# A two-layer retention and neighbourhood-attention block on one core: weighings of ada rows pinned to their written place on VectorE

## The chip, the cores and the metric

The kernel runs on one core of a Trainium2 chip. The core has a matrix engine (TensorE, PE in the profile), a vector engine (VectorE, DVE), an activation engine (ScalarE, ACT), a general engine (GpSimd, POOL) and a queue engine that here only issues transfers (SyncE, SP). Each of them works through its own list of instructions in the order of that list and waits where an operand is not there yet. The metric is the device time of one execution in microseconds, as a median over runs; lower is better.

## The reference

The computation is a small diffusion transformer: 256 latent tokens and 256 context tokens of width 1024, two layers, float32.

Every layer first makes modulation vectors: `silu(c) @ ada_w[i] + ada_b[i]` for the latent tokens and the same with `c_ctx` for the context, six vectors of 1024 each (shift, scale and gate for the mixer, and again for the MLP). Then

- layer 0, the retention mixer: q, k, v and a gate are projected from the modulated tokens by `ret_w_in` (1024 x 6144); four heads with 256 columns of q and k and 512 of v; scores weighted by a decay over distance, forward and backward, the context first and then the latent tokens with the context's state; each head's output is normalized over its 512 columns, multiplied by `silu(gate)`, and all heads go through `ret_w_o` (2048 x 1024);
- a layer norm over `ALPHA * x + gate * y`, a modulation, an MLP with squared ReLU (1024 to 4096 to 1024), and a second layer norm;
- layer 1, the neighbourhood mixer with 32 heads, and again an MLP, for the latent tokens alone.

The output is the 256 latent tokens.

## The kernel before

All matrix products run as three products of float32r pieces. A weight comes into one of four `raw` buffers (`rawp`, L138), ScalarE copies it into a `hi` tile, VectorE subtracts to get `lo`, and `mm3` (L174) multiplies hi by hi, hi by lo and lo by hi. `fetch` (L255) issues the load and the copy, `lows` (L277) the subtraction, and `take` (L282) does both until five units are there ahead of use (`WB = 5`, L135). Activations are split the same way (`split`, L170).

**Order.** The kernel is written with tiles, and a planner turns the text into one list for each engine. It goes by its own model of times: an engine takes, of the instructions whose inputs the model takes as ready, the one that is written first. So an instruction may be planned ahead of others that are written before it. `InOrder` (L74) wraps the engines: with `on` set, each instruction is tied behind the one written just before it on the same engine. SyncE is tied at the start (`PIN`), so loads are issued in written order; the opening stage and the passages around the layer norms are tied on other engines too. The tie goes one way: an untied instruction written later may still be planned earlier than a tied one.

**Layer 0, mixer (L1060 on).** All 512 tokens are handled together, in four token tiles of 128. A loop runs over the four heads. In head 0, q and v have been made by the opening stage. For each head: `proj_T` for q and k; a loop of four steps for the values (L1090); `masked_scores` (L1123); the gate of token tiles 0 and 1; the product of scores and values with its statistics for four token tiles (`po`, `bs`, `on`); the gates of token tiles 2 and 3 in one pass (`gates`, L1106), in whose midst `to_oT` (L1191) turns the head's output of token tiles 0 and 1 on TensorE (`pT`), copies it (`oh`, ScalarE) and takes the low part (`ol`, VectorE). Then comes the output projection: two halves of 512 columns, four token tiles each, 12 matmuls a tile into `pw`; `gated` (L736) multiplies by the gate row into `acc` on VectorE and `add_to` adds it to the residual on GpSimd. The turns of token tiles 2 and 3 stand after tiles 0 and 1 of the first half. In head 3 the output projection is a passage of its own in tied order, with the layer norm.

**The background stream (L532).** The modulation vectors that are needed later are made beside all this. `bg()` (L600) advances a generator by one step. A step loads the next row block of `ada_w` into a `raw` buffer (128 x 2 x 512, 512 KB) and deals with the block loaded before. For the first eight blocks TensorE does the product. For the other 24 blocks of layer 0, VectorE multiplies by a column of `silu(c)` and accumulates:

```python
for kk in range(2):
    for t in range(nt):
        weigh(spare(t), raw[:, kk, :], t, 2 * (n % 4) + kk, n % 4 == 0 and kk == 0)
```

That is four weighings a block (`strips<-rawa` in the profile, since the sums lie in the spare part of the strip tiles). After every fourth block a further step folds the two sums into `red` (`folded`, L456), and after eight the columns or the gate row are finished at the next call (`flush`). So each third of the modulation vectors takes ten calls, and the stream of layer 0 takes 39 calls (`bg_max`). For layer 1 the stream weighs into `acc` tiles, beside the MLP of layer 0.

The calls before: head 0 makes four in `proj_T`, two in the first gate, one after the scores, two in the second gate (nine in all), then one at the middle and one at the end of the second pair of gates, one behind it (L1205), and four in the output projection, after token tiles 1 and 3 of each half. Heads 1 and 2 make three in the loop of values (steps 1 to 3), one after each of gates 0 and 1, one at L1205, and four in the output projection. Head 3 makes the last three in its loop of values.

Of the kernel before, what the change touches and what calls it, by code (L numbers as in the profile page):

```python
# [104 lines left out]
def kernel(  # L105
# [23 lines left out]
    pe, act, dve, pool, sp = (  # L129
        InOrder(tc, getattr(nc, e), e in PIN)  # L130
        for e in ("tensor", "scalar", "vector", "gpsimd", "sync")
    )
# [19 lines left out]
    def nm(s):  # L152
        uid[0] += 1
        return f"{s}_{uid[0]}"

    def bank(s="ps"):
        return psp.tile([P, 512], F32, tag="ps", name=nm(s))
# [8 lines left out]
    def tsl(t):  # L166
        return slice(t * P, (t + 1) * P)
# [259 lines left out]
    def ada_bias(l, offs, nb):  # L427
        brow = scr("brow")
        ab = ada_b[l]
        for i in range(2):  # L430
            sp.dma_start(
                out=brow[64 * i : 64 * i + 64, :nb],
                in_=bass.AP(ab.tensor, ab.offset + offs[i], [[nb, 2], [0, 32], [1, nb]]),
            )
        return brow

    def ada_mm(pr, k, nb, rhs):

        lhsT = cT[:, k, :, :].rearrange("p a t -> p (a t)")
        for j in range(4):  # L440
            pe.matmul(
                pr[32 * j : 32 * j + 32, 0:nb],
                lhsT=lhsT,
                rhs=rhs(j),
                start=(k == 0),
                stop=(k == KC - 1),
                tile_position=(0, 32 * j),
            )

    def ada_row(pr, brow, nb, p0=0, p1=P, row=None):  # L450
        if row is None:
            row = smp.tile([P, 256], F32, tag="row", name=nm("row"), bufs=1)
        dve.tensor_add(out=row[p0:p1, :nb], in0=pr[p0:p1, 0:nb], in1=brow[p0:p1, :nb])
        return row

    def folded(red, acc, t, c0, n):  # L456

        dve.tensor_reduce(
            out=red[:, t, c0 // 32 : (c0 + n) // 32], in_=acc.rearrange("p (b i) -> p b i", i=32),
            axis=mybir.AxisListType.X, op=ALU.add, apply_transpose=True,  # L460
        )
# [44 lines left out]
    def on_pe(l, w, part):  # L506
        return (l, w, part) == (0, 0, 2)

    def bg_load(l, w, part, offs, n):

        if l == 1 or w == 0:
            return ada_load(l, n, offs)
        raw = rawp.tile([P, 2, 512], F32, tag="raw", name=nm("rawa"))
        w_ap = ada_w[l][256 * (n % 4) : 256 * (n % 4) + 256, offs[n // 4] : offs[n // 4] + 512]
        sp.dma_start(out=raw[:], in_=w_ap.rearrange("(k p) n -> p k n", p=P))
        return raw

    def weigh(acc, raw, t, k, first):

        col = scol[:, t, k : k + 1]  # L520
        if first:
            dve.tensor_scalar_mul(out=acc, in0=raw, scalar1=col)
        else:
            dve.scalar_tensor_tensor(out=acc, in0=raw, scalar=col, in1=acc, op0=ALU.mult, op1=ALU.add)
# [3 lines left out]
    def flush():  # L528
        while due:
            due.pop(0)()  # L530

    def bg_stream():  # L532


        plan = []
        for l, w, part in (
            [(0, 0, 2), (0, 1, 0), (0, 1, 1), (0, 1, 2)]
            + [(1, 0, 0), (1, 0, 1), (1, 0, 2), (1, 1, 0), (1, 1, 1), (1, 1, 2)]
        ):
            sh, sc, g = 3 * w * D, (3 * w + 1) * D, (3 * w + 2) * D  # L540
            offs = (sh + 512 * part, sc + 512 * part) if part < 2 else (g, g + 512)
            for n in range(KC):
                plan.append((l, w, part, offs, n))
        nxt = bg_load(*plan[0])
        yield
        for step, (l, w, part, offs, n) in enumerate(plan):
            raw = nxt
            if step + 1 < len(plan):
                nxt = bg_load(*plan[step + 1])

            nt = 2 if l == 0 or (w == 0 and part < 2) else 1
            if on_pe(l, w, part):
                if n == 0:
                    pr = bank("pada")
                if n == KC - 2:
                    brow = ada_bias(l, offs, 256)
                ada_mm(pr, n, 256, lambda j: raw[:, j // 2, (j % 2) * 256 : (j % 2 + 1) * 256])
                if n == KC - 1:
                    row = ada_row(pr, brow, 256)
                    for t in range(2):  # L560
                        pool.dma_start(
                            out=grow[l, w][t].rearrange("(j c) -> j c", j=4), in_=row[t:P:32, :]
                        )
                yield
                continue
            if n == 0:
                red = smp.tile([P, 2, 32], F32, tag="red", name=nm("red"), bufs=2)
            if l == 0:
                for kk in range(2):
                    for t in range(nt):  # L570
                        weigh(spare(t), raw[:, kk, :], t, 2 * (n % 4) + kk, n % 4 == 0 and kk == 0)
                if n % 4 == 3:
                    yield
                    for t in range(nt):
                        folded(red, spare(t), t, 512 * (n // 4), 512)
            else:
                if n == 0:
                    acc = slot(S_VL, [P, 2, D], F32, "acc")
                for t in range(nt):

                    dve.on = n == 0 and (w, part) == (0, 0)
                    weigh(acc[:, t], raw[:].rearrange("p a n -> p (a n)"), t, n, n == 0)
                    dve.on = False
                if n == KC - 1:
                    for t in range(nt):
                        folded(red, acc[:, t], t, 0, D)
            if n == KC - 1:
                if part < 2:
                    due.append(lambda a=(l, w, red, 4 * part, nt): ada_columns(*a))
                else:  # L590
                    due.append(lambda a=(l, w, red, nt): ada_gate(*a))
            yield
# [7 lines left out]
    def bg(n=1):  # L600
        for _ in range(n):
            if bg_done[0] < bg_max[0]:
                flush()
                bg_done[0] += 1
                next(bgs, None)
# [224 lines left out]
    def spare(t):  # L830
        return strips[t][:, 1536:2048]
# [238 lines left out]
    for h in range(RH):  # L1070
        last = h == RH - 1
        if h == 0:
            qkh = slot(S_TH, [P, 4, NT], F32R, "qkh")
            qkl = slot(S_TL, [P, 4, NT], F32R, "qkl")
            vh = slot(S_VH, [P, 4, DV], F32R, "vh")
            vl = slot(S_VL, [P, 4, DV], F32R, "vl")
            rotate(pq, qkh[:, 0:2], qkl[:, 0:2], True)
            evac_v(pv, vh, vl)
            act.on = True
            for a in range(2):  # L1080
                act.mul(out=RR[a][:], in_=RR[a][:], mul=ALPHA)
            act.on = False
            proj_T(qkh[:, 2:4], qkl[:, 2:4], True)
        else:
            qkh = slot(S_TH, [P, 4, NT], F32R, "qkh")
            qkl = slot(S_TL, [P, 4, NT], F32R, "qkl")
            proj_T(qkh[:, 0:2], qkl[:, 0:2])
            proj_T(qkh[:, 2:4], qkl[:, 2:4])
            vh = slot(S_VH, [P, 4, DV], F32R, "vh")
            vl = slot(S_VL, [P, 4, DV], F32R, "vl")  # L1090
            pv = [bank("pv") for _ in range(4)]
            for u in range(4):
                ((wh, wl),) = take(1)
                for t in range(4):
                    for kk in range(2):
                        k = 2 * u + kk
                        mm3(pv[t][:], hs(k, t * P, (t + 1) * P), (wh[:, kk, :], wl[:, kk, :]), k == 0, k == KC - 1)
                if u:
                    bg()
            evac_v(pv, vh, vl)  # L1100
        qh, ql, kh, kl = qkh[:, 0:2], qkl[:, 0:2], qkh[:, 2:4], qkl[:, 2:4]

# [88 lines left out]
        def to_oT(t):  # L1191
            pT = bank("pT")
            for i in range(4):
                pe.transpose(pT[:, tsl(i)], gs[:, t, tsl(i)], ident)
            pv_ = pT[:].rearrange("p (k t) -> p k t", k=4)
            act.copy(out=oh[:, :, tsl(t)], in_=pv_)
            dve.tensor_sub(out=ol[:, :, tsl(t)], in0=pv_, in1=oh[:, :, tsl(t)].bitcast(F32))

        between = {4: lambda: to_oT(0), 5: lambda: to_oT(1)}
        for t, pg in zip((2, 3), gates((2, 3), between)):  # L1200
            sg = scr("sg")
            act.activation(out=sg[:], in_=pg[:], func=AF.Silu)
            pool.tensor_mul(out=gs[:, t, :], in0=sg[:], in1=gs[:, t, :])
            if t == 2:
                bg()  # L1205

        bg_until(9)
        first_gate()
# [1014 lines left out]
```

## Time and profile before

| | before |
|---|---|
| median of 3 runs | 1208.73 us (1206.9 to 1209.21) |
| the profiled execution | 1205.15 us, span 1203.4 us |
| mean granted TensorE clock | 0.997 |
| TensorE busy | 1176.1 us (98%) |
| VectorE busy | 825.5 us (69%) |
| ScalarE busy | 477.8 us (40%) |
| GpSimd busy | 255.0 us (21%) |
| weighings of layer 0 | 96, from 89.5 to 373.5 us |
| low parts of the head outputs (`ol`) | 16, from 115.0 to 437.8 us |

A line of a timeline has the start, the duration, the engine, the line of the source, the operation, `out<-in` by the names of the tiles, the shapes, and how many instructions are merged; in brackets stands the idle time of that engine just before, and what ended it. Nearly all instructions have the line of the wrapper, L84, so groups are told apart by their tiles. A line of the waits has the waiting engine and tile, the releaser, the microseconds in sum, the number of waits, and the longest. A line of the windows has busy time of PE, PEld, DVE, ACT and POOL (with counts), then the granted clock, the share of the DMA engines and GB/s.

### The profile page before, as it was taken

Reading aid. Unit: us, or ns where it says so; the run is one execution under the profiler, and the core shown is the slowest. Engines: PE = TensorE matmul, PEld = TensorE weight load, DVE = VectorE, ACT = ScalarE, POOL = GpSimd, SP = SyncE. Lnnn points to the kernel's source line nnn. Section 1 sums busy time; section 2 is a strip of 40 time slices with the busy share of each in tenths; the row PEclk is TensorE's granted clock in tenths of the full one; section 3 lists DMA queues with packets and bytes.
Section 4 is the critical chain, followed back from the end, with each engine's and each line's share of the span. In section 5 each row is a group of like instructions: output and inputs, shape, how many; then the busy total and the mean of one; then the engine's idle time right before and its main releaser. Section 6 shows DMA issues by size and latency. Waiting matters only on the chain.

```text
span 1203.4 us, 17830 instructions
## 1 busy us (share of the span) xinstructions
PE 1176.1 (98%) x6867; PEld 986.4 (82%) x6867; DVE 825.5 (69%) x1307; ACT 477.8 (40%) x809; POOL 255.0 (21%) x390
## 2 busy tenths in 40 slices
PE   7999899999999999999999999999999999999997
PEld 5777788788878888888888888889778878999886
DVE  3778676768576478667876675578576688787445
ACT  3562122323222246442122333227466665666341
POOL 1103400420340131491203000122444431000001
PEclk9999999999999999999999999999999999999999
DMA  9766443344143123856566655546244335566660
GB/s 302 225 228 193 144 134 107 105 133 165 62 154 117 59 82 117 263 113 195 170 197 204 211 189 196 185 150 204 80 144 133 103 115 162 182 211 202 236 210 36
DMA packets 130265, 193.16 MB, mean 161 GB/s; under 512 B 9676, under 2 KB 73332, under 8 KB 130180
## 3 DMA queue, kind: packets, MB, share of 16 engines
q1 hardware_dynamic: 121796, 179.02, 46.1%
q0 software_dynamic: 7232, 10.44, 3.9%
q10 hardware_dynamic: 1152, 2.56, 0.7%
q8 instruction: 54, 0.88, 0.3%
q14 instruction: 31, 0.25, 0.1%
HBM read 187.15 MB, written 5.75 MB: 160 GB/s over the span
## 4 chain that ended last, share of the span: by engine, by line
PE 82%; DVE 8%; DMA 4%; issue 2%; ACT 2%; POOL 1%; SPq 0%; DVEq 0%; ACTq 0%; POOLq 0%
PE p L84 40%; PE pq L84 7%; PE pv L84 7%; PE pn L84 5%; PE pg L84 5%; PE pw L84 4%; PE pnv L84 4%; DMA rawa<-in_ada_w_dram 2%; DVE lo L84 2%; PE po L84 2%; PE ppt L84 2%; PE pS L84 1%; PE pqk L84 1%; PE pada L84 1%; PE pav L84 1%
## 5 line engine op out<-in xcount | busy, mean ns | idle before, releaser
L84 ACT CAST hi<-raw 128x1024 fp32r<-128x1024 f32 (+2 forms) x228 | 231.9, 1032 | 323.6 <-PE p L84 123.4
L84 DVE TENSOR_TENSOR lo<-raw,hi 128x1024 fp32r<-128x1024 f32 (+2 forms) x228 | 274.0, 1214 | 109.5 <-ACT hi L84 109.1
L84 PE MATMUL p<-hi,hid 128*128 128x512 f32 (+1 forms) x832 | 241.8, 374 | 0.0
L84 PEld LDWEIGHTS p<-hi,hid 128*128 128x128 f32 x832 | 152.2, 188 | 27.7
L84 PE MATMUL p<-hTh,lo 128*128 128x256 f32 (+1 forms) x512 | 167.5, 327 | 1.9 <-DVE lo L84 1.9
L84 PE MATMUL p<-hTh,hi 128*128 128x256 f32 (+1 forms) x512 | 167.9, 328 | 0.2 <-ACT hTh L84 0.2
L84 PE MATMUL p<-hTl,hi 128*128 128x256 f32 (+1 forms) x512 | 167.3, 327 | 0.4 <-DVE hTl L84 0.4
L84 PE MATMUL p<-lo,hid 128*128 128x512 f32 (+1 forms) x416 | 155.3, 373 | 0.0
L84 DVE SCALAR_TENSOR_TENSOR acc<-rawa,scol,acc 128x1024 f32<-128x1024 f32 x56 | 74.7, 1344 | 66.0 <-DMA rawa<-in_ada_w_dram 66.0
L84 POOL TENSOR_TENSOR R<-R,acc 128x512 f32<-128x512 f32 x40 | 63.2, 1596 | 209.9 <-DVE acc L84 209.8
L84 PEld LDWEIGHTS p<-hTh,lo 128*128 128x128 f32 x512 | 96.4, 188 | 11.2 <-DVE lo L84 2.5
L84 PEld LDWEIGHTS p<-hTl,hi 128*128 128x128 f32 x512 | 96.4, 188 | 9.5 <-DVE hTl L84 0.8
L84 PEld LDWEIGHTS p<-hTh,hi 128*128 128x128 f32 x512 | 96.3, 188 | 9.2 <-ACT hTh L84 0.4
L84 PEld LDWEIGHTS p<-lo,hid 128*128 128x128 f32 x416 | 78.4, 188 | 13.6
L84 ACT CAST hid<-r 128x256 fp32r<-128x256 f32 (+1 forms) x64 | 32.0, 500 | 109.9 <-DVE r L84 109.9
L84 DVE SCALAR_TENSOR_TENSOR strips<-rawa,scol,strips 128x512 f32<-128x512 f32 x84 | 66.8, 830 | 9.8 <-DMA rawa<-in_ada_w_dram 9.7
L84 POOL TENSOR_TENSOR rstd<-rstd,misc 128x1 f32<-128x1 f32 x28 | 18.8, 672 | 208.5 <-DVE rstd L84 207.2
L84 PE MATMUL pw<-hi,ol 128*128 128x512 f32 x128 | 51.0, 398 | 6.5 <-DVE ol L84 6.5
L84 ACT ACTIVATE s<-s,mn 128x512 f32<-128x512 f32 x64 | 45.5, 713 | 26.2 <-DVE mn L84 26.2
L84 PE MATMUL pw<-hi,oh 128*128 128x512 f32 x128 | 51.6, 403 | 0.0
L84 PE MATMUL pg<-hi,hTh 128*128 128x512 f32 x128 | 51.3, 401 | 0.0
L84 PE MATMUL pw<-lo,oh 128*128 128x512 f32 x128 | 50.5, 394 | 0.0
(238 smaller groups left out, 2288.3 us busy)
## 6 DMA issues: line engine op xcount, KB each, us to landing
raw<-in_mlp_w_dram SPq DMA_DIRECT2D x128, 512.0 KB, 4.5
rawa<-in_ada_w_dram SPq DMA_DIRECT2D x80, 512.0 KB, 3.9
raw<-in_ret_w_in_dram SPq DMA_DIRECT2D x42, 512.0 KB, 3.5
raw<-in_nat_w_in_dram SPq DMA_DIRECT2D x24, 512.0 KB, 5.1
rawq<-in_ada_w_dram SPq DMA_DIRECT2D x16, 512.0 KB, 6.4
raw<-in_ret_w_o_dram SPq DMA_DIRECT2D x16, 512.0 KB, 3.5
bias<-rpb_rows POOLq DMA_DIRECT2D x32, 128.0 KB, 2.9
raw<-in_nat_w_o_dram SPq DMA_DIRECT2D x8, 512.0 KB, 4.2
```

What stands on the lines that cost most here:

```text
L84: r = f(*args, **kwargs)
```

## The change

Three edits. The weighings of layer 0 are tied in written order on VectorE. The subtraction that makes `ol` is tied too, with the setting that was there restored behind it. And `bg()` is called in all four steps of the loop of values of heads 1 to 3, while the call behind the second pair of gates, in every head, is gone.

```diff
             if l == 0:
+                dve.on = True
                 for kk in range(2):
                     for t in range(nt):
                         weigh(spare(t), raw[:, kk, :], t, 2 * (n % 4) + kk, n % 4 == 0 and kk == 0)
+                dve.on = False
                 if n % 4 == 3:
                     yield
                     for t in range(nt):
...
                         mm3(pv[t][:], hs(k, t * P, (t + 1) * P), (wh[:, kk, :], wl[:, kk, :]), k == 0, k == KC - 1)
-                if u:
-                    bg()
+                bg()
             evac_v(pv, vh, vl)
...
             act.copy(out=oh[:, :, tsl(t)], in_=pv_)
+            pinned, dve.on = dve.on, True
             dve.tensor_sub(out=ol[:, :, tsl(t)], in0=pv_, in1=oh[:, :, tsl(t)].bitcast(F32))
+            dve.on = pinned
...
             pool.tensor_mul(out=gs[:, t, :], in0=sg[:], in1=gs[:, t, :])
-            if t == 2:
-                bg()
```

The calls after: head 0 makes one fewer, heads 1 and 2 as many as before with the first at step 0 of the loop of values, and head 3 makes the last four there. The count of instructions and of bytes is the same.

## The prediction

> **What bounds the kernel now.** I read the busy table first, then TensorE's waits, then the timelines of TensorE and VectorE around each wait, and last the issues of SyncE and the idle of the helpers. The busy table and TensorE's longest waits:
>
> ```profile
> span 1203.4 us, 17830 instructions
> PE 1176.1 (98%) x6867; PEld 986.4 (82%) x6867; DVE 825.5 (69%) x1307; ACT 477.8 (40%) x809; POOL 255.0 (21%) x390
> PE pw L84 <- DVE ol L84: 6.5, 4, 2.8
> PE p L84 <- DVE lo L84: 1.9, 3, 0.8
> ```
>
> TensorE works 1176.1 of 1203.4 us, so 27.3 us of idle is all that any reordering elsewhere can win, plus slow clock. The largest wait of the whole run is the third line: matmuls of the output projection (`pw`) wait four times, 6.5 us in sum, for `ol`, the low part of the turned head output. That is the tile that the change pins. The four on TensorE, in order of time (start, duration, [idle before <- releaser]), the first with the last matmul ahead of it:
>
> ```profile
> 119.27 0.40 PE L84 MATMUL pw<-lo,oh 128*128 128x512 f32 x1
> 121.53 0.50 PE L84 MATMUL pw<-hi,ol 128*128 128x512 f32 x1 [1.85 <-DVE ol L84]
> 130.52 0.61 PE L84 MATMUL pw<-hi,ol 128*128 128x512 f32 x1 [2.80 <-DVE ol L84]
> 134.27 0.39 PE L84 MATMUL pw<-hi,ol 128*128 128x512 f32 x1
> 134.49 0.39 PE L84 MATMUL pw<-hi,oh 128*128 128x512 f32 x1
> 235.37 0.50 PE L84 MATMUL pw<-hi,ol 128*128 128x512 f32 x1 [1.27 <-DVE ol L84]
> 337.99 0.50 PE L84 MATMUL pw<-hi,ol 128*128 128x512 f32 x1 [0.62 <-DVE ol L84]
> ```
>
> Two are in head 0, one in head 1, one in head 2. What VectorE did instead:
>
> ```profile
> 117.13 1.94 DVE L84 TENSOR_SCALAR strips<-rawa,scol 128x512 f32<-128x512 f32 x2 [1.42 <-DMA rawa<-in_ada_w_dram]
> ...
> 120.79 0.68 DVE L84 TENSOR_TENSOR ol<-pT,oh 128x512 fp32r<-128x512 f32 x1
> 121.39 0.73 DVE L84 SCALAR_TENSOR_TENSOR strips<-rawa,scol,strips 128x512 f32<-128x512 f32 x1
> ...
> 123.19 0.68 DVE L84 TENSOR_TENSOR acc<-pw,G 128x512 f32<-128x512 f32 x1
> 123.79 0.67 DVE L84 TENSOR_TENSOR ol<-pT,oh 128x512 fp32r<-128x512 f32 x1
> 127.19 2.08 DVE L84 SCALAR_TENSOR_TENSOR strips<-rawa,scol,strips 128x512 f32<-128x512 f32 x3 [2.73 <-DMA rawa<-in_ada_w_dram]
> 129.18 0.68 DVE L84 TENSOR_TENSOR acc<-pw,G 128x512 f32<-128x512 f32 x1
> 129.78 0.68 DVE L84 TENSOR_TENSOR ol<-pT,oh 128x512 fp32r<-128x512 f32 x1
> ...
> 232.04 2.08 DVE L84 SCALAR_TENSOR_TENSOR strips<-rawa,scol,strips 128x512 f32<-128x512 f32 x3 [1.30 <-DMA rawa<-in_ada_w_dram]
> ```
>
> The weighings (`strips<-rawa`) stand on VectorE ahead of work that the text of the kernel puts before them, and at 127.19 the engine sits idle 2.73 us for a row of ada weights, weighs three times (2.08 us), and only then makes `acc` and the `ol` on which TensorE has stood since 127.7. Head 1 repeats it at 232.04. By the calls of `bg()` the weighings at 117 to 135 belong to the second half of the output projection and to head 1's loop of values: they ran early because nothing held them.
>
> **The change part by part.** *Weighings held in order.* Each of the 96 weighings of layer 0 now follows what was written before it on VectorE. No instruction is added. In head 0 the row whose call stands in the output projection (after `ol` of token tile 3) can no longer stand before that `ol`; so the 2.73 us of idle and the 2.08 us of weighing leave its path. *`ol` held in order*: it stands behind the `acc` or the `ol` written before it, and the next weighings behind it. *The call moved*: the call at line 1205, behind the second pair of gates and ahead of the output projection, goes, and the loop of values of heads 1 to 3 gets one at its first step, so the output projection starts with no weighing in front of it in heads 1 and 2. In head 0 a call is lost, and the stream runs one call later until head 1's loop of values; the last call falls in head 3's loop either way.
>
> The terms, TensorE time saved if all four waits go: 1.85 + 2.80 + 1.27 + 0.62 = 6.54 us. To this comes the clock behind the 2.80 us wait:
>
> ```profile
> 130.00:132.00 2.00, 1.48 (x4) 1.18 (x5) 2.00 (x3) 0.00 (x0) 1.21 (x1) 0.69 0.00 0
> 132.00:134.00 2.00, 2.00 (x6) 1.52 (x6) 2.00 (x4) 1.04 (x1) 0.24 (x1) 0.50 0.52 160
> 134.00:136.00 2.00, 2.00 (x10) 1.67 (x9) 2.00 (x3) 1.05 (x1) 1.50 (x1) 0.96 0.29 102
> ```
>
> The third column from the right is the granted clock: 0.69, 0.50, 0.96. From 130.52 to 134.27 nine matmuls started in 3.75 us; at the 0.22 us of the step from 134.27 to 134.49 they take 1.98 us, so 1.75 us (rounded to 1.7) go with the wait. Sum 8.2 us.
>
> [...]
>
> What is moved also has to fit elsewhere. One weighing costs 0.75 us undisturbed:
>
> ```profile
> L84 DVE SCALAR_TENSOR_TENSOR strips<-rawa,scol,strips x84: 718/745/1780, 92.1 to 373.5; 128x512 f32<-128x512 f32 x84
> 116.06 2.73 POOL L84 TENSOR_TENSOR gs<-sg,gs 128x512 f32<-128x512 f32 x2 [4.65 <-ACT sg L84]
> 224.63 3.84 POOL L84 TENSOR_TENSOR gs<-sg,gs 128x512 f32<-128x512 f32 x2 [7.30 <-ACT sg L84]
> 179.37 1.22 DVE L84 TENSOR_TENSOR lo<-raw,hi 128x1024 fp32r<-128x1024 f32 x1 [2.78 <-ACT hi L84]
> 181.38 4.30 DVE L84 SCALAR_TENSOR_TENSOR strips<-rawa,scol,strips 128x512 f32<-128x512 f32 x6 [0.79 <-DMA rawa<-in_ada_w_dram]
> 207.32 0.70 DVE L84 BATCH_NORM_STATS2 bs<-po 128x6 f32<-128x512 f32 x1 [7.99 <-PE po L84]
> ```
>
> The four weighings put into the loop of values are 4 x 0.75 = 3.0 us; VectorE idled 2.78 + 0.79 = 3.57 us in that loop of head 1, and the low parts of weights made there are for the gates, written after the scores. I cost them at nothing; without that cover they would be 3.0 us a head at most. The two rows of the calls after gate tiles 0 and 1 now run where they are written: 8 x 0.75 = 6.0 us, against 7.99 us of idle before `bs`. Nothing.
>
> *Raw buffers.* Four are shared by weights and ada rows, and SyncE issues in written order. A row held until its call keeps its buffer:
>
> ```profile
> 89.15 4.74 SPq L84 DMA_DIRECT2D rawa<-in_ada_w_dram  x3
> 93.98 5.62 SPq L84 DMA_DIRECT2D raw<-in_ret_w_o_dram  x3
> rawa<-in_ada_w_dram SPq DMA_DIRECT2D x80, 512.0 KB, 3.9
> raw<-in_ret_w_o_dram SPq DMA_DIRECT2D x16, 512.0 KB, 3.5
> 186.85 5.88 SPq L84 DMA_DIRECT2D raw<-in_ret_w_o_dram  x3
> 116.62 1.04 ACT L84 CAST hi<-raw 128x1024 fp32r<-128x1024 f32 x1
> 119.24 0.59 ACT L84 CAST oh<-pT 128x512 fp32r<-128x512 f32 x1 [1.57 <-PE pT L84]
> ```
>
> Before, three rows and then three output weights left by 99.6 us, since the rows were weighed at once. Now three rows wait for their calls, which I estimate at about 108, 115 and 125 us. One output weight gets the fourth buffer; the second and third leave at about 111, when the first row is weighed, land 3.5 us later, and are needed for the second half, at about 128: covered. The fourth (the next head's q) leaves at about 118, lands at 122; its copy and its low part could be planned just ahead of `oh` and `ol` of tile 3, which would then wait: from nothing to 2.0 us (landing 122, copy 1.04, low part 1.2, `acc` 0.6, `ol` 0.68 gives 125.5 to 126.5; the matmul wants it at about 125). In head 0 a weighing also still meets POOL's two products (2.73 us there; where weighings met them in head 1, 3.84), which is up to 1.1 us on the chain to the next transposes, with about 1 us of slack. I take 0.7 of these 0 to 3.1 us, near the low end, because heads 1 and 2 have cover: the three output weights of head 1 left from 186.85 on, and the two rows whose buffers they may now wait for are weighed by about 205 (199.3, where VectorE's idle before `bs` began, and 6.0); landed by 209, they are wanted from 225 on.
>
> Sum: 8.2 - 0.7 = 7.5 us. The profiled run took 1205.15 us (span 1203.4 and 1.75 around it), 3.58 below the median of the runs, 1208.73. So 1197.6 against the profiled run, and on the median's scale 1208.73 - 7.5 = 1201.2 us. TensorE is the bound from 63 us to the end, so what it saves early stays saved.
>
> **The rivals.** *The waits shrink but come back elsewhere.* `ol` is then late behind low parts of weights or `acc` that were behind the weighings before. For it: the order of everything unpinned is still the planner's, which believes loads earlier than they land (the 2.73 us above). Against it: `ol` now stands directly behind the `acc` of one tile earlier, and that is ready about 1.6 us before it is needed. It would keep the two small waits and half of the first, with the clock gained: 8.2 - (1.27 + 0.62 + 0.9) = 5.4, or, if the 2.80 us gap only shrinks to 1.85, 2.7 us: 1203.3 to 1206.0.
>
> *No change.* Pinning does not move `ol`, or the planner shifts something after head 3 by as much. Each instruction added to a fixed order can only be asked to wait longer. Within 0.2% (2.4 us, about what a measurement of this kernel can tell from no change): 1206.3 to 1211.1.
>
> *Slower: ScalarE stands in front of a held load.* A row pinned behind the output chain holds a raw buffer; the next weight's load leaves that much later; ScalarE, which copies the weight (`hi`) and makes `oh` on one queue, waits for it with `oh` behind it, and so do `ol` and TensorE. For it: 116.62 and 119.24 above stand 1.6 us apart in that order. Against: by the estimate above the loads of heads 1 and 2 have some 16 us to spare (209 against 225). It decides from 8.2 / 3 = 2.7 us a head on; with a wait of one load (3.5 us) and the 1.7 us of clock behind it in each of three heads it costs 15.6 - 8.2 = 7.4 us: 1216.
>
> [...]
>
> **How the numbers follow.** Forecast with the waits gone 0.55 (own range 1198.7 to 1204.2: gains of 8.2 to 5, and the runs' spread, 1206.9 to 1209.21, about the median; the small clock gain, 0.04, is in it), partial 0.19, no change 0.10, slower 0.16. Faster is 0.74, same 0.10, slower 0.16. The range runs from 1198.7 to 1209.5: it takes in the forecast, the partial case and most of no change, and leaves out the slower case.
>
> **What would show it.** Right: no wait of `pw` for `ol` over 0.7 us, a granted clock of 1.00 through the output projection of head 0; no weighing on VectorE between the first and the last `ol` of heads 1 and 2; the first weighings at about 108 us instead of 89; the idle before the first `bs` of head 1 down from 7.99 to about 2. Wrong: `ol` behind a `lo` that waits for `hi`, ScalarE's `hi` waiting for a load between two `oh`, new waits of `pv`, `pS` or `po`, or the same TensorE idle moved past 470 us.

## The result, and the profile after

The changed kernel takes 1201.29 us (median of 5 runs, 1199.77 to 1201.89) against 1207.70 us for the kernel before (5 runs, 1206.28 to 1209.21). The ratio is 0.9946, with a 95% interval from 0.9935 to 0.9957: 0.54% faster. The forecast was 1201.2 us.

The two profiled executions are nearer to each other than the medians: spans of 1199.5 and 1203.4 us, 3.9 us apart, where the medians are 6.4 apart. The profiled run of the kernel before, 1205.15 us, lies below all five of its timed runs. So these two traces can account for 3.9 us; the rest is between runs.

From the page of the changed kernel, the span and the busy table, and from its waits those of TensorE:

```profile
span 1199.5 us, 17825 instructions
PE 1176.4 (98%) x6867; PEld 987.8 (82%) x6867; DVE 832.7 (69%) x1307; ACT 477.6 (40%) x809; POOL 250.9 (21%) x390
```

```profile
PE p L84 <- DVE lo L84: 3.0, 3, 1.7
PE pT L84 <- POOL gs L84: 1.9, 1, 1.9
...
PE pw L84 <- DVE ol L84: 0.5, 1, 0.5
```

The wait of `pw` for `ol` fell from 6.5 us in four to 0.5 in one. A new one stands in the second line: the transposes `pT` of the output projection wait 1.9 us for `gs`, the product of GpSimd. By stretches, first the changed kernel, then the kernel before:

```profile
93.00:125.00 32.00, 30.13 (x134) 24.43 (x131) 18.59 (x27) 7.33 (x10) 11.05 (x16) 0.95 0.37 117
125.00:205.00 80.00, 79.55 (x365) 65.52 (x364) 63.58 (x96) 21.44 (x31) 12.72 (x8) 1.00 0.48 151
205.00:315.00 110.00, 110.00 (x507) 91.03 (x506) 81.24 (x123) 28.40 (x41) 25.32 (x31) 1.00 0.38 115
315.00:400.00 85.00, 85.00 (x390) 70.61 (x389) 66.59 (x95) 27.20 (x39) 14.19 (x12) 1.00 0.45 136
```

```profile
93.00:125.00 32.00, 30.14 (x143) 24.66 (x140) 27.54 (x40) 8.00 (x11) 12.29 (x17) 1.00 0.61 190
125.00:205.00 80.00, 77.20 (x345) 63.37 (x344) 56.93 (x89) 20.72 (x31) 11.44 (x8) 0.98 0.41 135
205.00:315.00 110.00, 108.73 (x500) 89.66 (x499) 76.65 (x118) 28.45 (x41) 24.83 (x28) 1.00 0.36 115
315.00:400.00 85.00, 84.38 (x386) 69.77 (x385) 59.36 (x88) 26.54 (x37) 19.58 (x16) 1.00 0.38 122
```

TensorE's idle in these four stretches was 1.86 + 2.80 + 1.27 + 0.62 = 6.55 us and is 1.87 + 0.45 = 2.32 us. Heads 1 and 2 have none left. Head 0 still has a stall and a slow clock, now in the first stretch (0.95). The saving in idle is 4.2 us.

A surer measure is the length of a stage. From the first matmul of the output projection (`pw`) to the first `pq` of the next head, TensorE takes 29.5, 24.3 and 23.6 us in heads 0 to 2 of the kernel before, and 27.1, 22.7 and 22.7 us in the changed kernel. The 22.7 us are the undisturbed length: no trace of this case shows a shorter one. So the kernel before lost 6.8 + 1.6 + 0.9 = 9.3 us there, more than its waits and its slow clock in sum (8.2 us), because a wait cost some 0.3 us here beyond the idle that is listed for it: in heads 1 and 2, where the clock stayed up, 1.27 and 0.62 us of idle made the projection 1.6 and 0.9 us longer. The changed kernel loses 4.4 us, all in head 0, and so saves 4.9 us. By the first transposes of the layer norm in head 3 (`pt`), it is 4.7 us ahead (437.62 against 442.35 us); 0.8 us is lost again behind that, where the waits of `p` for `lo` grew from 1.2 to 2.2 us.

Head 0 on VectorE, and from head 1 the two `ol` of the output projection and the idle before the first `bs`:

```profile
109.74 0.87 DVE L84 TENSOR_SCALAR strips<-rawa,scol 128x512 f32<-128x512 f32 x2
110.53 1.41 DVE L84 SCALAR_TENSOR_TENSOR strips<-rawa,scol,strips 128x512 f32<-128x512 f32 x2
...
117.12 1.22 DVE L84 TENSOR_TENSOR lo<-raw,hi 128x1024 fp32r<-128x1024 f32 x1 [3.45 <-ACT hi L84]
118.26 0.68 DVE L84 TENSOR_TENSOR ol<-pT,oh 128x512 fp32r<-128x512 f32 x1
118.86 4.77 DVE L84 SCALAR_TENSOR_TENSOR strips<-rawa,scol,strips 128x512 f32<-128x512 f32 x4
...
126.42 0.68 DVE L84 TENSOR_TENSOR ol<-pT,oh 128x512 fp32r<-128x512 f32 x1
...
127.62 0.68 DVE L84 TENSOR_TENSOR ol<-pT,oh 128x512 fp32r<-128x512 f32 x1
128.22 3.39 DVE L84 SCALAR_TENSOR_TENSOR strips<-rawa,scol,strips 128x512 f32<-128x512 f32 x4
```

```profile
205.08 0.70 DVE L84 BATCH_NORM_STATS2 bs<-po 128x6 f32<-128x512 f32 x1 [3.42 <-PE po L84]
...
226.55 0.68 DVE L84 TENSOR_TENSOR ol<-pT,oh 128x512 fp32r<-128x512 f32 x1
...
229.32 0.69 DVE L84 TENSOR_TENSOR ol<-pT,oh 128x512 fp32r<-128x512 f32 x1 [0.36 <-ACT oh L84]
229.93 2.93 DVE L84 SCALAR_TENSOR_TENSOR strips<-rawa,scol,strips 128x512 f32<-128x512 f32 x4
```

The first weighing starts at 109.74 (89.49 before), and in head 1 the weighings follow the last `ol`, at 229.93. The weighings after gate tiles 0 and 1 have moved into the idle before `bs`, which fell from 7.99 to 3.42 us. But the second `ol` of head 0, which wants only a transpose done by 113.4, is made at 118.26. The reason is on ScalarE, and behind it on SyncE (the last line is SyncE's longest wait between 92 and 120 us):

```profile
111.68 0.59 ACT L84 CAST oh<-pT 128x512 fp32r<-128x512 f32 x1 [3.48 <-PE pT L84]
116.03 1.05 ACT L84 CAST hi<-raw 128x1024 fp32r<-128x1024 f32 x1 [3.77 <-DMA raw<-in_ret_w_o_dram]
116.99 0.58 ACT L84 CAST oh<-pT 128x512 fp32r<-128x512 f32 x1
117.76 1.05 ACT L84 CAST hi<-raw 128x1024 fp32r<-128x1024 f32 x1 [0.19 <-DMA raw<-in_ret_w_o_dram]
118.72 1.07 ACT L84 ACTIVATE sg<-pg 128x512 f32<-128x512 f32 x2
121.97 1.05 ACT L84 CAST hi<-raw 128x1024 fp32r<-128x1024 f32 x1 [2.18 <-DMA raw<-in_ret_w_in_dram]
```

```profile
89.31 3.89 SPq L84 DMA_DIRECT2D rawa<-in_ada_w_dram  x2
93.29 20.18 SPq L84 DMA_DIRECT2D raw<-in_ret_w_o_dram  x3
...
SPq L84 <- DVE strips L84: 18.2, 1, 18.2
```

```profile
120.78 0.90 PE L84 MATMUL pT<-cst,gs 128*128 128x128 f32 x4 [1.87 <-POOL gs L84]
```

Three output weights left between 93.98 and 99.60 us before; now their issues are spread over 20.18 us, because held rows have three of the four `raw` buffers: SyncE waits 18.2 us for the weighings of the first row. The second weight leaves at 111.96, when they end, and the third at 113.10. ScalarE has the copy of the second of these weights ahead of the second `oh` and of `sg`, and stands 3.77 us for the load. `sg` comes at 118.72 (115.39 before), GpSimd makes `gs` from it, and the transposes, due at 118.9, start at 120.78.

### The profile page after: what moved, and what is told of

Read it like the earlier page. It is cut to its first block, busy times and chain, and to the rows that moved or that the text cites. A ratio compares the mean times of both kernels' runs of the same rounds, so it can differ in the third digit from the quotient of the medians.

```text
span 1199.5 us, 17825 instructions
## 1 busy us (share of the span) xinstructions
PE 1176.4 (98%) x6867; PEld 987.8 (82%) x6867; DVE 832.7 (69%) x1307; ACT 477.6 (40%) x809; POOL 250.9 (21%) x390
## 4 chain that ended last, share of the span: by engine, by line
PE 87%; DVE 7%; DMA 2%; ACT 2%; issue 2%; POOL 1%; DVEq 0%; ACTq 0%; POOLq 0%; SPq 0%
PE p L84 40%; PE pq L84 7%; PE pv L84 7%; PE pg L84 7%; PE pw L84 6%; PE pn L84 5%; PE pnv L84 4%; PE po L84 2%; DVE lo L84 2%; PE pada L84 2%; PE ppt L84 2%; PE pS L84 1%; PE pqk L84 1%; PE pav L84 1%; DMA raw<-in_mlp_w_dram 1%
## 5 line engine op out<-in xcount | busy, mean ns | idle before, releaser
L84 DVE TENSOR_TENSOR lo<-raw,hi 128x1024 fp32r<-128x1024 f32 (+2 forms) x228 | 277.3, 1229 | 100.7 <-ACT hi L84 100.3
L84 POOL TENSOR_TENSOR R<-R,acc 128x512 f32<-128x512 f32 x40 | 60.3, 1521 | 205.2 <-DVE acc L84 204.9
L84 DVE SCALAR_TENSOR_TENSOR strips<-rawa,scol,strips 128x512 f32<-128x512 f32 x84 | 64.3, 822 | 0.0
L84 DVE TENSOR_TENSOR hid<-r,hid 128x256 fp32r<-128x256 f32 (+1 forms) x64 | 34.5, 539 | 23.0 <-ACT hid L84 22.9
```

The source lines that it names most:

```text
L84: r = f(*args, **kwargs)
```

## The experiments

The theory that stood at the end of the forecast: tying the weighings takes them off the path of `ol`, the moved call keeps the way free, and the rest, put at 0.7 us, is head 0's buffers and VectorE's load there. What is left in head 0 after the change is 1.87 + 0.45 us of idle and 1.7 us of slow clock, 4.0 us (4.4 by the length of the stage), so the first question was which of the two causes it has.

**The tie of `ol`.** It needed no run: with and without this edit, the lists of all five engines are the same instruction by instruction. The planner put `ol` behind the instruction written before it in any case. This part of the change does nothing.

**The ties on the weighings alone.**

```diff
             if l == 0:
+                dve.on = True
                 for kk in range(2):
...
+                dve.on = False
```

> The kernel before with the weighings tied, and nothing else: the calls stay where they were, so one call stands between the second pair of gates and the output projection. Theory of the forecast (the ties do the work, the moved call only keeps the way free): heads 1 and 2 lose their waits on the low part (1.27 and 0.62 us), but in head 0 two rows, eight weighings of 0.75 us or more, stand in a row between the second and the third ol, which is needed about 4 us after the second. So TensorE stands some 3 us there, the clock falls behind it (1.7 us), and the waits of the changed kernel in head 0 come on top: 1206.5 us, between 1204 and 1209. Rival (the ties alone bring all of it and the moved call is idle): 1201.5 us.

Measured: 1206.56 us (1204.47 to 1208.43), ratio 0.9999 (0.9989 to 1.0009). No change. VectorE, ScalarE and TensorE in head 0 of this kernel:

```profile
119.70 6.85 DVE L84 SCALAR_TENSOR_TENSOR strips<-rawa,scol,strips 128x512 f32<-128x512 f32 x8
```

```profile
127.40 1.04 ACT L84 CAST hi<-raw 128x1024 fp32r<-128x1024 f32 x1 [3.01 <-DMA raw<-in_ret_w_o_dram]
128.35 0.58 ACT L84 CAST oh<-pT 128x512 fp32r<-128x512 f32 x1
```

```profile
128.98 0.50 PE L84 MATMUL pw<-hi,oh 128*128 128x512 f32 x1 [3.81 <-ACT oh L84]
```

Eight weighings stand in a row, as expected, and TensorE waits 3.81 us in one piece with the clock at 0.68 from 130 to 135 us. But what it waits for is `oh`, and not only the `ol` behind the weighings, which is done at about the same time (128.9 us). ScalarE stands 3.01 us for an output weight that left at 123.9 us, when the first of the two rows had been weighed and gave its buffer back, with `oh` behind the copy. So a held buffer delays this kernel too. And in heads 1 and 2 waits of 1.00 us for `ol` stay, where the expectation had them gone (1.27 and 0.62 before). The ties without the moved call save next to nothing in any head.

**The moved call alone.**

```diff
-                if u:
-                    bg()
+                bg()
...
-            if t == 2:
-                bg()
```

> The kernel before with the calls moved, and nothing tied. The planner still puts weighings ahead of acc and ol by its own times. Theory of the forecast: the waits of TensorE for ol stay about as before, some 4 to 7 us in sum with the slow clock behind one: 1204 to 1208 us, 1206 as one number. Rival (moving the call is what helps): 1201.5 us.

Measured: 1204.82 us (1203.60 to 1206.55), ratio 0.9982 (0.9973 to 0.9990), inside the range that the theory gave, and a small gain all the same. TensorE's waits from 63 to 470 us have this line:

```profile
PE pw L84 <- DVE ol L84: 6.0, 7, 1.4
```

The sum of the waits for `ol` is nearly the old one (6.5 us), but in seven pieces of at most 1.4 us instead of four with one of 2.80. The clock stays at 1.00 in every slice of head 0, so the 1.7 us of slow clock are saved. By the length of the stages head 0 gains 3.0 us (26.5 against 29.5), and heads 1 and 2 lose 0.5 and 1.1 us (24.8 each).

**The first two rows of head 0 left untied.** The changed kernel otherwise; run twice.

```diff
-                dve.on = True
+                dve.on = bg_done[0] > 11
```

> The changed kernel with the first two rows of head 0 (the calls inside the second pair of gates) left untied, so that they are weighed as early as in the kernel before and give their raw buffers back. Theory A, held buffers: what is left of the stalls in head 0 (1.87 us before the transpose, 0.45 us before a matmul on the low part, and some 1.7 us of slow clock) comes from output weights that leave late because rows hold three of the four raw buffers; then ScalarE waits for no load between its two oh copies, all three go, and the time is about 4.0 us under that of the changed kernel: 1197.3 us. Theory B, VectorE's burden: the eight weighings in the middle of the chain are themselves what delays it; then the gain is the same 4 us, but ScalarE's waits for a load stay. If neither, 1201.3 us.

> The kernel with the first two rows of head 0 untied, again, as the measure for the run beside it: 1198.3 us, ratio 0.992 to the kernel before, and no wait of TensorE over 0.8 us between 63 and 470 us.

Measured: 1198.28 us (1196.88 to 1199.41), ratio 0.9919 (0.9902 to 0.9936), and the second time 1197.25 us (1194.90 to 1197.83), ratio 0.9915 (0.9900 to 0.9931). This version beats both kernels. ScalarE waits for no load between the two `oh` (here from the first run), and no wait of TensorE for `ol` or `gs` is left between 63 and 470 us:

```profile
112.34 0.59 ACT L84 CAST oh<-pT 128x512 fp32r<-128x512 f32 x1 [0.76 <-PE pT L84]
113.68 1.05 ACT L84 CAST hi<-raw 128x1024 fp32r<-128x1024 f32 x1 [0.75 <-PE pg L84]
114.64 0.57 ACT L84 CAST oh<-pT 128x512 fp32r<-128x512 f32 x1
116.21 1.34 ACT L84 ACTIVATE sg<-pg 128x512 f32<-128x512 f32 x2 [0.99 <-PE pg L84]
```

The changed kernel beside it on the same chip:

> The changed kernel itself, beside the other three and the kernel before on one chip: 1201.3 us, ratio 0.9946 to the kernel before. A reading of how far a profiled run stands from the median.

Measured: 1201.91 us (1200.01 to 1203.79), ratio 0.9951 (0.9935 to 0.9968). The two rows are worth 3.6 us. In its trace head 0 had two waits, 1.75 us for `gs` and 2.05 us for `ol`, and the clock fell behind the second (its mean was 0.68 from 125 to 130 us): 5.9 us lost by the length of the stage, against 4.4 in the first trace. So the loss and its split change from run to run.

**Half of each row held.** Of the two rows, the weighings for the first token kind run early and those for the second stay tied.

```diff
-                dve.on = True
-                for kk in range(2):
-                    for t in range(nt):
-                        weigh(...)
+                early = bg_done[0] <= 11
+                order = [(kk, t) for t in (1, 0) for kk in range(2)] if early else [(kk, t) for kk in range(2) for t in range(2)]
+                for kk, t in order:
+                    dve.on = t == 1 or not early
+                    weigh(...)
```

> As the first, but of those two rows the weighings for the second token kind stay tied to their written place and only those for the first kind run early. The buffers are held as long as in the changed kernel, and VectorE has half of the eight weighings there (four of about 0.75 us). Theory A: all of the stall stays, 1201.3 us, with ScalarE waiting some 3 us for a load ahead of the second oh. Theory B: half of the stall or less stays, 1197.3 to 1199.5 us.

Measured: 1198.83 us (1197.00 to 1202.38), ratio 0.9928 (0.9909 to 0.9946). ScalarE:

```profile
115.07 1.05 ACT L84 CAST hi<-raw 128x1024 fp32r<-128x1024 f32 x1 [6.48 <-DMA raw<-in_ret_w_o_dram]
```

The copy still waits for its load, yet TensorE lost only 0.9 us for `ol` and 0.2 for `gs`, and no clock. That speaks against theory A in its plain form, that the held buffers alone make the whole stall, but does not refute it: with only two weighings of the row tied, the buffer came back sooner, and the copy starts 0.96 us earlier than in the changed kernel (116.03).

**Stand-ins for the weighings.** The rows run early, and eight weighings of a table into a spare tile stand where the rows stood.

```diff
+                if bg_done[0] <= 11:
+                    dum = scr("dum")
+                    for _ in range(4):
+                        dve.scalar_tensor_tensor(out=dum[:], in0=strips[0][:, :512], ...)
+                    dve.on = False
```

> As the first (rows weighed early, buffers free), but eight weighings of a table into a spare tile, which nothing reads, stand tied where the two rows stood in the changed kernel. VectorE is as burdened as in the changed kernel and no buffer is held. Theory A: as the first, about 1197.5 us, at most 1 us more. Theory B: 1201 us, with TensorE's stall of some 2 us in the output projection of head 0 back.

Measured: 1199.17 us (1198.23 to 1201.26), ratio 0.9931 (0.9915 to 0.9948). One wait for `ol`, of 1.7 us, came back, without a slow clock, and none for `gs`. So the weighings alone, with no buffer held, make a part of the stall and not all of it: neither theory stands alone.

**A tiny tied read of each row.** It keeps the buffer until the call and costs VectorE 0.14 us.

```diff
+                if bg_done[0] <= 11:
+                    keep = smp.tile([P, 1], F32, tag="keep", name=nm("keep"), bufs=1)
+                    dve.tensor_copy(out=keep[:], in_=raw[:, 0, 0:1])
+                    dve.on = False
```

> As the kernel with the first two rows untied, but one copy of a single column of each row, into a tile that nothing reads, is tied where the row stood in the changed kernel. So the raw buffers are held as long as there and VectorE has next to nothing (about 0.1 us) to do for it. Theory A (held buffers alone make the stall): TensorE waits 1.9 us before a transpose and the clock falls behind it, 1201 us. Theory B (the weighings on VectorE alone): no wait, 1198.3 us. Theory C (it takes both; each alone leaves 1 to 2 us of wait and no slow clock, as the two runs with half of the weighings and with stand-ins suggest): up to 1.2 us of wait, clock 1.00, 1198.8 us.

Measured: 1197.60 us (1197.11 to 1198.36), ratio 0.9921 (0.9908 to 0.9935); 0.4 us of wait for `gs`, clock 1.00. VectorE and ScalarE:

```profile
109.22 0.14 DVE L84 COPY keep<-rawa 128x1 f32<-128x1 f32 x1
```

```profile
112.96 1.05 ACT L84 CAST hi<-raw 128x1024 fp32r<-128x1024 f32 x1 [5.28 <-PE pT L84]
```

The stall is gone, but so is a part of the hold: the read is over at 109.36, where the four weighings of the changed kernel end at 111.9, and the copy starts at 112.96 instead of 116.03. The length of the weighing belongs to the hold. So this run does not separate the two causes. The next two take a row at a time.

**One row at a time.** Only the second row untied, and only the first. The second adds to the same sums as the first, so in the first of these runs it moves forward only to stand right behind it:

```diff
-                dve.on = True
+                dve.on = bg_done[0] != 11
```

> The changed kernel with only the second row of head 0 (the call at the end of the second pair of gates) untied. The first row stays tied behind the last normalization of the chain, so the second, which adds to the same sums, can come no earlier than behind it: all eight weighings stand there in a row, before the first ol, and both buffers come free by about 115 us (the second at 123.6 in the changed kernel). If the first row's buffer, which comes free only when it is weighed, makes the load, ScalarE's copy and so the transpose late, TensorE still waits about 1.9 us there; the second low part then meets an empty VectorE and the wait of 0.5 us goes: 1199.5 to 1201.5 us. If it is the eight weighings between the second ol and the third, the wait goes altogether: 1198.3 us.

Measured: 1201.53 us (1200.20 to 1202.62), ratio 0.9957 (0.9944 to 0.9971): nothing gained over the changed kernel. TensorE, ScalarE, and the clock in the stretch:

```profile
122.78 1.12 PE L84 MATMUL pT<-cst,gs 128*128 128x128 f32 x4 [2.81 <-POOL gs L84]
```

```profile
116.55 1.05 ACT L84 CAST hi<-raw 128x1024 fp32r<-128x1024 f32 x1 [3.27 <-DMA raw<-in_ret_w_o_dram]
...
119.30 1.05 ACT L84 CAST hi<-raw 128x1024 fp32r<-128x1024 f32 x1 [1.21 <-DMA raw<-in_ret_w_o_dram]
```

```profile
120.00:125.00 5.00, 2.22 (x8) 1.93 (x9) 3.44 (x3) 2.96 (x5) 3.03 (x2) 0.71 0.77 240
```

```diff
-                dve.on = True
+                dve.on = bg_done[0] != 10
```

> The changed kernel with only the first row of head 0 (the call in the middle of the second pair of gates) untied; the second row stays tied behind the second ol. The first output weight that was late now has its buffer in time, so ScalarE waits for no load ahead of the second oh and the wait before the transpose goes; the four weighings and GpSimd's two products still meet, so that a wait of the third tile for its ol of up to 1.7 us, as with the stand-ins, can stay, and no slow clock: 1198.5 to 1200 us. If the second row's weighings were the cause, 1201.3 us with the wait before the transpose.

Measured: 1199.96 us (1198.74 to 1200.50), ratio 0.9944 (0.9931 to 0.9956). TensorE and ScalarE:

```profile
119.78 0.66 PE L84 MATMUL pT<-cst,gs 128*128 128x128 f32 x4 [0.85 <-POOL gs L84]
...
125.68 0.50 PE L84 MATMUL pw<-hi,ol 128*128 128x512 f32 x1 [1.59 <-DVE ol L84]
```

```profile
116.27 1.05 ACT L84 CAST hi<-raw 128x1024 fp32r<-128x1024 f32 x1 [3.99 <-PE pg L84]
```

Each held row keeps a load back that ScalarE stands for. With the first tied and the second right behind it, the second and third output weights leave at 112.97 and 115.62 us, and ScalarE waits for both ahead of `sg`; so `gs` and the transposes come late, the wait is 2.81 us, and the clock falls. With the first free and the second tied, the second weight leaves at 94.4 us and only the third is late: it leaves at 112.67 and lands at 116.20, and its copy at 116.27 stands ahead of the second `oh` and of `sg` (the profile names `pg`, whose last matmul ended at the same time). In the run with both rows free that weight left at 97.3 and its copy started at 113.68. That is the 0.85 us for `gs`, which was not expected. The second row does another harm as well: its four weighings stand between the second and the third `ol`, and 1.59 us before a matmul on `ol` remain (1.7 with the stand-ins), without a slow clock. How the loss of the changed kernel divides between the two rows is not shown, because the first run does not remove the second row's weighings from the chain. No run has a fifth `raw` buffer, which would test the hold by itself.

**All runs by the length of the stage.** Output projection of heads 0, 1 and 2 in each trace, what they lost over 3 x 22.7 us, and the median against that of the kernel before in the same session, all in us:

| kernel | head 0 | head 1 | head 2 | lost | below before |
|---|---|---|---|---|---|
| before | 29.5 | 24.3 | 23.6 | 9.3 | |
| changed | 27.1 | 22.7 | 22.7 | 4.4 | 6.4 |
| changed, again | 28.6 | 22.7 | 22.7 | 5.9 | 4.6 |
| weighings tied only | 29.2 | 24.0 | 24.0 | 9.1 | 0.4 |
| call moved only | 26.5 | 24.8 | 24.8 | 8.0 | 2.2 |
| first two rows untied | 22.7 | 22.7 | 22.7 | 0.0 | 8.3 |
| the same, again | 22.7 | 22.7 | 22.7 | 0.0 | 9.7 |
| half of each row held | 24.7 | 22.7 | 22.7 | 2.0 | 7.7 |
| stand-ins | 25.0 | 22.7 | 22.7 | 2.3 | 7.4 |
| tiny tied read | 23.4 | 22.7 | 22.7 | 0.7 | 9.4 |
| second row untied | 27.1 | 22.7 | 22.7 | 4.4 | 5.2 |
| first row untied | 25.6 | 22.7 | 22.7 | 2.9 | 6.8 |

What a kernel gains goes with what its projections lose: its median is lower by about as much as its loss is below 9.3 us, within 1.5 us. Each trace is one execution, and the second trace of the changed kernel shows how far one can stand from another (1.5 us).

## Why the prediction was right, and where it was not

- **What bounds the kernel**: right. TensorE's waits for `ol` were what the change could take, and the 2.80, 1.27 and 0.62 us went. In heads 1 and 2 nothing came in their place.
- **The sum of 8.2 us for all four waits**: only reached with the first two rows untied. Those two runs stand 8.3 us (1206.55 to 1198.28) and 9.7 us (1206.99 to 1197.25) below the kernel before. The sum was a little small: it counts the idle alone, and by the length of the stages 9.3 us were to be had.
- **The clock term of 1.7 us**: the slow clock was real and can be saved (it is gone from the trace of the moved call alone, whose waits have nearly the old sum and whose median is 2.2 us lower). In the changed kernel it was not saved: it moved to another stall in head 0. The subtraction behind the term is off by a little, without effect: 3.75 - 1.98 is 1.77 us, not 1.75. The forecast's chances also count a small clock gain, 0.04: slow matmuls that stay when the wait goes. No run shows that. In the output projection of head 0 the slow clock stood behind waits of 1.87 us and more in every trace that has one, and in the traces without such a wait, as that of the moved call alone, the clock read 1.00.
- **What is left in head 0, taken at 0.7 of 0 to 3.1 us**: this term failed. It measured 4.0 us (1.87 + 0.45 and 1.7 of clock), and 5.5 us in the second trace (1.75 + 2.05 and 1.7), beyond its upper end, which had no clock in it. The step behind it said that the second and third output weights, leaving at about 111, were covered because the product needs them at about 128. They did leave then and they were not needed earlier, but their copies stand on ScalarE ahead of `oh` and `sg`, which were. I had written that order down for the fourth weight, and as the slower rival, and had not carried it to the second. The rival's mechanism is thus what happened, in one head, not three. Of the signs that the prediction named for being wrong, one is in the trace: a `hi` that waits for a load between two `oh`. And one of its signs for being right is missing: the clock in head 0 did not stay at 1.00.
- **The moved call costs nothing in the loop of values; the two rows after the gates fit into the idle before `bs`**: right; no wait of TensorE there, and 7.99 us of idle became 3.42.
- **`ol` held in order**: it was given no price of its own, and has none; it changes nothing.
- **1201.2 us against 1201.29**: the direction and the main mechanism were earned, the closeness is luck. The gain was set at 7.5 us; the traces show 3.9 (4.9 in the output projections) and the medians 6.4, or 4.6 beside the kernel before of the second chip session (1206.55 to 1201.91). It was taken off a median of three runs, 1208.73, which is 1.7 us above the median of 23 later runs (1206.99). The two errors run against each other.

## What to carry to other kernels

When background work is tied to its written place, what it holds (here one of four load buffers) is tied with it, so ask which load that delays and what stands behind that load's first consumer on its own queue; the date on which the product is needed is not enough. Ties and call places work together: here the ties alone gave nothing, the moved call alone 0.2%, both 0.5%, and both without the two rows that hold buffers 0.8%. And a chain of short waits can cost less than one long wait, if the long one brings the slow clock (1.7 us behind the wait of 2.80 us): the moved call alone lost 8.0 us over seven waits of 6.0 us in sum, the kernel before 9.3 us over four of 6.5. But each wait had a price beyond its idle here, some 0.3 us, so cutting one into pieces was no gain by itself: with the moved call alone heads 1 and 2 became longer, 24.8 us against 24.3 and 23.6.

## What the runs showed of the hardware

In the output projections, TensorE's clock fell behind gaps of 2.80 us (before, 0.50 from 132 to 134 us), 1.87 us (changed, 0.50 in the slice below), 2.05 us (changed, again, 0.68 from 125 to 130 us), 2.81 us (second row untied, 0.71 from 120 to 125 us) and 3.81 us (weighings tied only, 0.68 from 130 to 135 us); it stayed at 1.00 behind 1.85 us (before), 1.75 us (changed, again), 1.59 us (first row untied), 1.7 us (stand-ins) and seven of up to 1.4 us (call moved only). From the changed kernel, the slices around the 1.87 us gap:

```profile
120.00:122.00 2.00, 1.22 (x6) 1.12 (x7) 2.00 (x2) 0.03 (x1) 2.00 (x2) 0.76 0.67 227
122.00:124.00 2.00, 2.00 (x6) 1.56 (x5) 2.00 (x3) 1.50 (x2) 0.41 (x1) 0.50 0.00 0
124.00:126.00 2.00, 2.00 (x12) 1.58 (x10) 2.00 (x3) 0.00 (x0) 0.55 (x1) 0.88 0.56 125
```

1.85 and 1.87 us fell on different sides, 0.02 us apart. What the clock goes by, no run here shows.
